# Score products with the keys' lo parts in a plane per head, over all 128 rows

## The chip, the cores and the metric

The kernel runs on one core of a Trainium2 chip, as one launch. The metric is the device time of one execution in microseconds, lower is better; the number given for a kernel is the median of its runs. The engines named here are TensorE (PE, with its weight loads shown apart as PEld), VectorE (DVE), ScalarE (ACT), GpSimd (POOL) and SyncE (SP), which issues most transfers.

## What is computed

Two decoder layers over 512 tokens of width 1024. Layer A is a gated short convolution, layer B a stick-breaking attention of 12 heads of 64 over keys and values made once; each layer also attends into 256 memory tokens with 4 heads of 64, and ends in a SwiGLU FFN. What the change touches are the two score products. In the reference they are:

```python
def memory_cross_attention(q, mem_k, mem_v):
    scale = 1.0 / math.sqrt(HEAD_DIM)
    s = jnp.einsum("bshd,bmhd->bhsm", q.astype(jnp.float32), mem_k.astype(jnp.float32)) * scale
    p = jax.nn.softmax(s, axis=-1)
...
def stick_breaking_attention(q, k, v):
    ...
        z = jnp.einsum("bhtd,bhsd->bhts", qb, kb) * scale
        log_not = jnp.where(causal, jax.nn.log_sigmoid(-z), 0.0)
        tail = lax.cumsum(log_not, axis=3, reverse=True) - log_not
        log_a = jax.nn.log_sigmoid(z) + tail
        a = jnp.where(causal, jnp.exp(log_a), 0.0)
        outs.append(jnp.einsum("bhts,bhsd->bhtd", a, vb))
```

## The kernel before

Every float32 operand of a product is held as two parts, hi (rounded to float32r) and lo (the rest), and a product is hi·hi + hi·lo + lo·hi, summed in PSUM. `mm` (L131 to 136) issues one matmul; all matmuls have line 132 in the profile, all transpositions line 139. `hi_of` (L143) makes a hi part on ScalarE and `lo_of` (L146) a lo part on VectorE.

A head has 64 features, so two heads share the 128 rows of a tile. `queries` (L414) writes for each head a plane `q[:, head]` of 128 rows: the head's own 64 rows hold the hi part, the other head's 64 rows hold the lo part. `keys` (L425) writes `kd[:, head]`, the hi part of the head's keys in both halves of the rows, and `kl`, the lo part, one plane in which each head has its own 64 rows. `scores_of` (L435) then makes a head's scores with two matmuls: queries (hi and lo) times `kd` over 128 rows, and queries hi times `kl` over the head's 64 rows alone.

`scores_of` has two callers. In `mem_attention`, `scores` makes for one head two token tiles of 256 memory scores, so four matmuls `sc` in a row; there are 8 such steps in each of the two layers. In layer B, `weigh` makes the scores `z` of one head and one query tile of 128 rows against 128, 256, 384 or 512 keys: two matmuls of `scores_of` and a third of 128 columns that adds the causal mask (`maskr`, `identr`, 128 rows). There are 12 heads of 4 query tiles, 48 steps. After `weigh`, ScalarE makes two sigmoids (L731, L732), VectorE a scan and a product (L734, L735), `turn` transposes the weights two steps later (`at`), and `weighted` multiplies them with the values (`av`).

The order of the work is a list of emission. `Lanes` counts columns of matmuls: a step of attention is put between the matmuls of a large product when so many columns have gone by (`STICK_PACE`, `MEM_PACE`), however long they took. Each engine then runs its list in order. The columns of both matmuls of `scores_of` are the same before and after the change. `kl` comes from a rotating pool of 3 buffers; the memory keys `k` of a pair are one tile of 3 planes (two of `kd`, one of lo). POOL has little to do: constants, the power -0.5 of each norm (`rstd_of`, L260) and the two zero columns ahead of each convolution input (`cu`, L565).

Of the kernel before, what the change touches and what calls it, by code (L numbers as in the profile page):

```python
# [9 lines left out]
F32 = mybir.dt.float32  # L10
F32R = mybir.dt.float32r
# [5 lines left out]
P = 128  # L17
# [15 lines left out]

# buffers
A_BUFS = 25
W_BUFS = 9
RAW_BUFS = 2
T_BUFS = 9
# column pairs of the FFN's hidden features that are held at a time
FF_GROUPS = ((0, 4), (4, 8), (8, 11))  # L40
# pieces of a weight that are held to finish one token tile after the other
TAIL = 3
# columns of matmuls between the steps of a generator (see Lanes)
STICK_PACE = 4900
MEM_PACE = 12000, 10000
TURN_PACE = 600
# columns of matmuls before a step that needs what other engines make
LAG_OUT = 8000
# [4 lines left out]
LAG_SECOND = 3000  # L53
# steps by which the transposition and the weighted sum of stick-breaking follow the weights
TURN_AFTER = 2
# [3 lines left out]
class Lanes:  # L59
    """Order of emission: generators whose steps are put between the matmuls of the large products.  # L60
    A step yields how many columns of matmuls are to come before its next one."""

# [40 lines left out]
def trunk(ctx: ExitStack, tc: tile.TileContext, x, mem, mix_norm, a_in, conv_w, b_in,  # L103
          kv_norm, w_kv_shared, w_mem_kv, w_o, ffn_norm, w_gate, w_up, w_down,
          mem_norm, final_norm, out):
    """Every float32 operand of a large product is held as two parts of 12 significant bits,
    hi = float32r(v) and lo = v - hi (exact), and a product is hi*hi + hi*lo + lo*hi, summed in
    float32 in PSUM."""
    nc = tc.nc
# [37 lines left out]

# [1 line left out]
    nw = [0]  # L149
# [21 lines left out]
    def cols(w, c0, raw=None):  # L171
        """w[:, c0:c0+256] -> two (hi, lo) pairs of 128 columns"""
        raw = load_cols(w, c0) if raw is None else raw
        return [lambda h=h: split(raw[:, :, h * P:(h + 1) * P], KT, P) for h in range(2)]

    def rows(w, pieces, c0, n):
        """pieces of consecutive row tiles of w[:, c0:c0+n], two pieces to a raw tile"""
        for i in range(0, len(pieces), 2):
            two = pieces[i:i + 2]
            nk = len(two[0])  # L180
            raw = raw_tile([P, 2 * nk, n])
            if len(two) == 2 and two[1][0] == two[0][-1] + 1:
                spans = [(0, two[0] + two[1])]
            else:
                spans = [(j * nk, kts) for j, kts in enumerate(two)]
            for at, kts in spans:
                nc.sync.dma_start(raw[:, at:at + len(kts), :],
                                  w[kts[0] * P:(kts[-1] + 1) * P, c0:c0 + n].rearrange("(k p) c -> p k c", p=P))
            for j, kts in enumerate(two):
                yield kts, split(raw[:, j * nk:j * nk + len(kts), :], len(kts), n)  # L190
# [5 lines left out]

# [1 line left out]
    ident = const.tile([P, P], F32, name="ident")  # L198
# [26 lines left out]
    def columns(src, n, name):  # L225
        """[n, 128] -> [128, n]"""
        b = att(f"tr_{name}")
        transpose(b[:, :n], src, ident[:n, :n])
        c = const.tile([P, n], F32, name=name)
        nc.vector.tensor_copy(c, b[:, :n])  # L230
        return c
# [6 lines left out]
    def load_table(func, after):  # L238
        """have ACT fetch the function's table once it has made `after`"""
        nc.scalar.activation(small.tile([P, 1], F32, tag="table", name=f"table_{func}"), after, func)  # L240

# [1 line left out]
    def sum_tile(name):  # L243
        return small.tile([P, 2], F32, tag="ss", name=f"ss_{name}")

    def square_sum(ss, xrow, hf, name, dve=False):
        """mean square, half of it"""
        row = xrow[:, hf * 512:(hf + 1) * 512]
        junk = tpool.tile([P, 512], BF16, tag="junk", name=f"junk_{name}{hf}", bufs=2)
        if dve:  # L250
            nc.vector.scalar_tensor_tensor(junk, row, 1.0 / D, row, ALU.mult, ALU.mult,
                                           accum_out=ss[:, hf:hf + 1])
        else:
            nc.scalar.activation(junk, row, AF.Square, scale=1.0 / 32.0, accum_out=ss[:, hf:hf + 1])
# [8 lines left out]
    class Feat:  # L263
        """[features, tokens], split, in tiles of 1024 columns"""

# [9 lines left out]
    class Normed:  # L275
        """feat = transposed (source * rstd) * gain for each (feat, gain) of `into`, two token tiles
        at a time"""

# [48 lines left out]

# [1 line left out]
    def three(dst, a, b, first, last):  # L329
        """dst (+)= a.T @ b for split a, b: each a function of HI, LO"""  # L330
        mm(dst, a(HI), b(HI), first, False)
        mm(dst, a(HI), b(LO), False, False)
        mm(dst, a(LO), b(HI), False, last)

    def by_feature(dst, w, feat, lo, hi):
        """dst[128 out, tokens lo:hi] = w.T @ feat"""
        for k in range(KT):
            three(dst, lambda hl: w[hl][:, k, :], lambda hl: feat.at(k, hl, lo, hi), k == 0, k == KT - 1)
            lanes.pump()

    class Opening:
        """the first four products on a feat whose token tiles come one after the other"""

# [20 lines left out]
    def by_token(w, pieces, c0, n, lhs, ntok, name, done, tail=1):  # L364
        """[tokens, n] = lhs.T @ w[:, c0:c0+n]; done(t, bank) at a token tile's end. The last
        `tail` pieces go token by token."""
        banks = [acc(f"{name}{t}") for t in range(ntok)]
# [17 lines left out]

# [1 line left out]
    def normed(t, src, into, name, dve):  # L387
# [25 lines left out]
    def queries(b, name):  # L413
        """two heads' queries, scaled, for matmuls over 128 rows: [:, head] = hi and lo of its 64 rows,  # L414
        hi at the head's own rows"""
        q = slot([P, 2, S], F32R, name)
# [8 lines left out]
    def keys(b, kd, kl):  # L425
        """two heads' keys: kd[:, head] = hi of its 64 rows, twice; kl = lo"""
        for hh in range(2):
            r = hh * HD
            own, other = slice(r, r + HD), slice(HD - r, P - r)
            hi_of(kd[own, hh, :], b[own, :])  # L430
            hi_of(kd[other, hh, :], b[own, :])
            lo_of(kl[own, :], b[own, :], kd[own, hh, :])

    def scores_of(dst, q, hh, t, kd, kl, last):
        """dst[token tile t, keys] = queries . keys of head hh"""  # L435
        own = slice(hh * HD, (hh + 1) * HD)
        mm(dst, q[:, hh, t * P:(t + 1) * P], kd, True, False)
        mm(dst, q[own, hh, t * P:(t + 1) * P], kl[own, :], False, last)

    def mem_kv(layer):  # L440
# [3 lines left out]
        for c, get in enumerate(cols(w, 0)):  # L444
            b = acc(f"mk{layer}{c}")
            by_feature(b[:, :M], get(), memT, 0, M)
            k = slot([P, 3, M], F32R, f"mk{layer}{c}")
            keys(b[:, :M], k[:, 0:2, :], k[:, 2, :])
            mk.append(k)
# [9 lines left out]

# [1 line left out]
    def stacked_pv(pv, r, yf, name):  # L461
        """pv rows 0:64 hold V_hi, 64:128 V_lo products: yf[r:r+64] = their sum"""
        tmp = t2([P, S], F32, f"pv_{name}")
# [9 lines left out]
    def mem_attention(qs, layer, ys, pace):  # L473
# [3 lines left out]
        def scores(head, tp):  # L477
            pair, nm = head // 2, f"{layer}{head}{tp}"
            sc = att(f"sc{nm}")
            for u in range(2):  # L480
                t = 2 * tp + u
                scores_of(sc[:, u * M:(u + 1) * M], qs[pair], head % 2, t, mk[pair][:, head % 2, :],
                          mk[pair][:, 2, :], True)
            sc3 = sc.rearrange("p (u m) -> p u m", u=2)
# [55 lines left out]

# [1 line left out]
    ymain = [None] * PAIRS  # L542
# [42 lines left out]

# [1 line left out]
    def residual(t, hf, b, ss, name):  # L587
# [21 lines left out]
    def out_proj_late(layer, ys, last, opening, then):  # L609
        """as out_proj, the first row tiles before the last ones are there"""  # L610
        for hf in range(2):
# [83 lines left out]

# [1 line left out]
    qs = [None] * PAIRS  # L697
# [5 lines left out]
    def values(g4):  # L703
        """V of heads 4*g4 .. 4*g4+3"""
        def done(t, b):
# [13 lines left out]
    def stick(pace):  # L719
        weight, aT, pvs, yfs = {}, {}, {}, {}  # L720

        def weigh(p, hh, i):
            """stick-breaking weights of query tile i, [t, s]"""
            q, (kd, kl) = qs[p], ks[p]
            n, nm = (i + 1) * P, f"{p}{hh}{i}"
            z = att(f"z{nm}")[:, :n]
            scores_of(z, q, hh, i, kd[:, hh, :n], kl[:, :n], False)
            mm(z[:, i * P:n], identr, maskr, False, True)
# [66 lines left out]
    for c2 in range(3):  # L795
# [3 lines left out]
        for c, get in enumerate(cols(w_kv_shared, c2 * 256)):  # L799
# [3 lines left out]
            kd = slot([P, 2, S], F32R, f"kd{p}")  # L803
            kl = tpool.tile([P, S], F32R, tag="kl", name=f"kl{p}", bufs=3)
            keys(b, kd, kl)
# [59 lines left out]
```

## Time and profile before

| | |
|---|---|
| median of 3 runs | 1195.9 us (1195.87 to 1196.12) |
| span of the profiled execution | 1193.9 us |
| PE busy | 1176.0 us, 98% |
| PEld busy | 986.9 us, 83% |
| DVE busy | 587.5 us, 49% |
| ACT busy | 478.9 us, 40% |
| POOL busy | 16.8 us, 1% |
| granted TensorE clock, mean | 0.998 |

A row of TensorE says when a matmul started and how long it took from there until its end; matmuls overlap, so what one costs the engine is the distance from its start to the start of the next. PEld is the load of the stationary operand that a matmul needs first. Times of day are us from the start of the span. Stick-breaking runs from about 664 to 810 us, the memory attention of layer A from 74 to 128 us, that of layer B from 603 to 650 us.

### The profile page before, as it was taken

What the parts mean: (1) busy time and instruction counts of PE and PEld (TensorE: products, weight loads), DVE (VectorE), ACT (ScalarE), POOL (GpSimd) and SP (SyncE); (2) the same over time, 40 slices, a digit from 0 to 9 for tenths busy, and PEclk for the clock granted to TensorE, in tenths of its full rate; (3) what the DMA queues carried; (4) which work ended last, traced back from release to release, by engine and by line L of the source; (5) the groups of instructions that cost most, each with busy time, mean ns of one, the idle gap of its engine ahead of it and who ended that gap; (6) DMA issues with size and microseconds to landing.
All of it is one profiled execution on the core that took longest, in us unless ns stands there. A gap on an engine that the chain in (4) does not pass through costs nothing.

```text
span 1193.9 us, 14463 instructions
## 1 busy us (share of the span) xinstructions
PE 1176.0 (98%) x5945; PEld 986.9 (83%) x5945; DVE 587.5 (49%) x853; ACT 478.9 (40%) x824; POOL 16.8 (1%) x37
## 2 busy tenths in 40 slices
PE   6999999999999999999999999999999999999997
PEld 6887888988888888888978888778988888888886
DVE  6657543533323333333777688887333333333334
ACT  7454523532213221223766576656332223222222
POOL 1000000000000000000000000001000000000000
PEclk9999999999999999999999999999999999999999
DMA  7332322242232422323231211022233242332321
GB/s 248 107 106 71 108 105 71 72 141 99 79 106 71 129 83 92 119 71 106 71 106 39 71 51 54 28 79 88 72 106 106 71 124 88 106 106 71 106 71 71
DMA packets 91118, 109.50 MB, mean 92 GB/s; under 512 B 2026, under 2 KB 73772, under 8 KB 91052
## 3 DMA queue, kind: packets, MB, share of 16 engines
q1 hardware_dynamic: 91019, 108.56, 28.0%
q8 instruction: 47, 0.77, 0.3%
q14 instruction: 20, 0.16, 0.0%
q10 hardware_dynamic: 32, 0.01, 0.0%
HBM read 106.46 MB, written 2.10 MB: 91 GB/s over the span
## 4 chain that ended last, share of the span: by engine, by line
PE 96%; ACT 1%; DVE 1%; issue 1%; POOL 0%; DMA 0%; POOLq 0%; SPq 0%; DVEq 0%; ACTq 0%
PE u L132 21%; PE d L132 20%; PE g L132 18%; PE o L132 6%; PE gu L132 3%; PE z L132 3%; PE v L132 3%; PE k L132 3%; PE bg L132 3%; PE q L132 2%; PE pb L132 2%; PE cg L132 2%; PE sc L132 1%; PE pa L132 1%; PE av L132 1%; PE at L139 1%
## 5 line engine op out<-in xcount | busy, mean ns | idle before, releaser
L146 DVE TENSOR_TENSOR wl<-raw,wh 128x1024 fp32r<-128x1024 f32 x196 | 239.8, 1224 | 437.7 <-PE u L132 178.5
L143 ACT ACTIVATE wh<-raw 128x1024 fp32r<-128x1024 f32 x196 | 207.5, 1060 | 385.3 <-PE d L132 101.8
L132 PE MATMUL d<-wh,hid 128*128 128x512 f32 x704 | 218.0, 389 | 0.0
L132 PEld LDWEIGHTS d<-wh,hid 128*128 128x128 f32 x704 | 132.2, 188 | 27.3
L132 PE MATMUL d<-wl,hid 128*128 128x512 f32 x352 | 136.9, 389 | 0.0
L132 PEld LDWEIGHTS d<-wl,hid 128*128 128x128 f32 x352 | 66.1, 188 | 13.7
L656 ACT ACTIVATE sg<-g 128x512 f32<-128x512 f32 x40 | 24.0, 600 | 117.2 <-PE g L132 117.2
L132 PE MATMUL g<-hffn0h,wh 128*128 128x512 f32 x160 | 62.3, 389 | 0.0
L132 PE MATMUL g<-hffn1h,wh 128*128 128x512 f32 x160 | 62.3, 389 | 0.0
L132 PE MATMUL g<-hffn0l,wh 128*128 128x512 f32 x160 | 62.3, 389 | 0.0
L132 PE MATMUL g<-hffn1l,wh 128*128 128x512 f32 x160 | 62.3, 389 | 0.0
L132 PE MATMUL g<-hffn0h,wl 128*128 128x512 f32 x160 | 62.2, 389 | 0.0
L132 PE MATMUL u<-hffn0h,wh 128*128 128x512 f32 x160 | 62.2, 389 | 0.0
L132 PE MATMUL u<-hffn0l,wh 128*128 128x512 f32 x160 | 62.2, 389 | 0.0
L132 PE MATMUL u<-hffn0h,wl 128*128 128x512 f32 x160 | 62.2, 389 | 0.0
L132 PE MATMUL g<-hffn1h,wl 128*128 128x512 f32 x160 | 62.2, 389 | 0.0
L132 PE MATMUL u<-hffn1h,wh 128*128 128x512 f32 x160 | 62.2, 389 | 0.0
L132 PE MATMUL u<-hffn1l,wh 128*128 128x512 f32 x160 | 62.2, 389 | 0.0
L132 PE MATMUL u<-hffn1h,wl 128*128 128x512 f32 x160 | 62.2, 389 | 0.0
L146 DVE TENSOR_TENSOR hid<-sg,hid 128x512 fp32r<-128x512 f32 x44 | 30.5, 693 | 33.3 <-ACT hid L143 33.3
L589 DVE TENSOR_TENSOR x<-d,x 128x512 f32<-128x512 f32 x48 | 33.1, 690 | 25.7 <-PE d L132 25.7
L734 DVE TENSOR_TENSOR_SCAN sn<-sn 128x127 f32<-128x127 f32 (+3 forms) x48 | 39.2, 818 | 13.4 <-ACT sn L731 12.7
(242 smaller groups left out, 2355.9 us busy)
## 6 DMA issues: line engine op xcount, KB each, us to landing
raw<-in_w_gate_dram SPq DMA_DIRECT2D x22, 1024.0 KB, 5.4
raw<-in_w_up_dram SPq DMA_DIRECT2D x22, 1024.0 KB, 5.5
raw<-in_w_down_dram SPq DMA_DIRECT2D x20, 1024.0 KB, 5.0
raw<-in_a_in_dram SPq DMA_DIRECT2D x8, 1024.0 KB, 5.1
raw<-in_w_o_dram SPq DMA_DIRECT2D x12, 512.0 KB, 3.9
raw<-in_w_kv_shared_dram SPq DMA_DIRECT2D x6, 1024.0 KB, 5.0
raw<-in_w_mem_kv_dram SPq DMA_DIRECT2D x4, 1024.0 KB, 5.1
raw<-in_b_in_dram SPq DMA_DIRECT2D x4, 1024.0 KB, 5.0
```

The costliest lines, as they stand in the source:

```text
L132: nc.tensor.matmul(dst, a, b, start=start, stop=stop)
L139: nc.tensor.transpose(dst, src, idn)
L143: nc.scalar.activation(dst, src, AF.Copy)
L146: nc.vector.tensor_tensor(dst, src, hi.bitcast(F32), ALU.subtract)
L589: nc.vector.tensor_tensor(part, b, part, ALU.add)
L656: nc.scalar.activation(sg, bg, AF.Silu)
L734: nc.vector.tensor_tensor_scan(back, back, back, 1.0, ALU.mult, ALU.bypass)
```

## The change

The lo part of the keys gets a plane per head, like the hi part: in plane `kl[:, head]` the head's own 64 rows hold the lo part and the other head's rows hold zeros. The second matmul of `scores_of` then takes the whole 128 rows of `q[:, head]` and of that plane; the lo parts of the queries, which stand in the other rows, meet zeros. The zeros are written once by POOL (`zero_rows`). In layer B three tiles of two planes (`key_lo`) are made ahead of the loop and used in turn; for the memory keys the tile `k` grows from 3 to 4 planes, and each of its four instances gets two MEMSETs. Comments that were dropped are left out of the diff.

```diff
+KL_BUFS = 3
...
     def keys(b, kd, kl):
...
-            lo_of(kl[own, :], b[own, :], kd[own, hh, :])
+            lo_of(kl[own, hh, :], b[own, :], kd[own, hh, :])
 
     def scores_of(dst, q, hh, t, kd, kl, last):
-        own = slice(hh * HD, (hh + 1) * HD)
         mm(dst, q[:, hh, t * P:(t + 1) * P], kd, True, False)
-        mm(dst, q[own, hh, t * P:(t + 1) * P], kl[own, :], False, last)
+        mm(dst, q[:, hh, t * P:(t + 1) * P], kl, False, last)
+
+    def zero_rows(kl):
+        for hh in range(2):
+            nc.gpsimd.memset(kl[HD - hh * HD:P - hh * HD, hh, :].bitcast(F32), 0.0)
...
-            k = slot([P, 3, M], F32R, f"mk{layer}{c}")
-            keys(b[:, :M], k[:, 0:2, :], k[:, 2, :])
+            k = slot([P, 4, M], F32R, f"mk{layer}{c}")
+            zero_rows(k[:, 2:4, :])
+            keys(b[:, :M], k[:, 0:2, :], k[:, 2:4, :])
...
-                          mk[pair][:, 2, :], True)
+                          mk[pair][:, 2 + head % 2, :], True)
...
+    key_lo = [const.tile([P, 2, S], F32R, name=f"kl{i}") for i in range(KL_BUFS)]
+    for kl in key_lo:
+        zero_rows(kl)
...
-            scores_of(z, q, hh, i, kd[:, hh, :n], kl[:, :n], False)
+            scores_of(z, q, hh, i, kd[:, hh, :n], kl[:, hh, :n], False)
...
-            kl = tpool.tile([P, S], F32R, tag="kl", name=f"kl{p}", bufs=3)
+            kl = key_lo[p % KL_BUFS]
```

The lists of PE, DVE, ACT and SP hold the same instructions in the same places before and after; only POOL's list changes, at two places. At the start of the program, POOL makes the powers for the norms of the four token tiles (`rstd_x0` to `rstd_x3`) and of the two memory tiles (`rstd_m0`, `rstd_m1`); a bracket names the engines (or the DMA queue) whose signal a row waits for. Before:

```order
L260 TENSOR_TENSOR rstd_x0_128<-ms_x0_126,minus_half_82 128x1 [waits DVE_49]
L260 TENSOR_TENSOR rstd_x1_140<-ms_x1_138,minus_half_82 128x1 [waits DVE_49]
L260 TENSOR_TENSOR rstd_x2_196<-ms_x2_194,minus_half_82 128x1 [waits DVE_49]
L260 TENSOR_TENSOR rstd_x3_208<-ms_x3_206,minus_half_82 128x1 [waits DVE_49]
L260 TENSOR_TENSOR rstd_m0_468<-ms_m0_466,minus_half_82 128x1 [waits DVE_49]
L260 TENSOR_TENSOR rstd_m1_480<-ms_m1_478,minus_half_82 128x1 [waits DVE_49]
```

After:

```order
L261 TENSOR_TENSOR rstd_x0_128<-ms_x0_126,minus_half_82 128x1 [waits DVE_49]
L261 TENSOR_TENSOR rstd_x1_140<-ms_x1_138,minus_half_82 128x1 [waits DVE_49]
L444 MEMSET kl0_4337 64x512 [waits Pool_49]
L444 MEMSET kl0_4337 64x512
L444 MEMSET kl1_4338 64x512 x2
L444 MEMSET kl2_4339 64x512 x2
L261 TENSOR_TENSOR rstd_x2_196<-ms_x2_194,minus_half_82 128x1 [waits DVE_49,Pool_49]
L261 TENSOR_TENSOR rstd_x3_208<-ms_x3_206,minus_half_82 128x1 [waits DVE_49]
```

The six MEMSETs of the layer-B planes, though written far down in the program, stand between the powers of the second and the third token tile. In layer A, POOL's list holds the zero columns `cu` of the six convolution inputs; before:

```order
L565 MEMSET cu1_601 128x2
L565 MEMSET cu2_1018 128x2 [waits DVE_49,PE_49]
L565 MEMSET cu3_1075 128x2 [waits DVE_49,PE_49]
L565 MEMSET cu4_1478 128x2 [waits DVE_49]
L565 MEMSET cu5_1513 128x2 [waits PE_49,Pool_49]
```

After, the MEMSETs of the memory keys `mk` stand among them (`mk00`, `mk01` of layer A, `mk10`, `mk11` of layer B):

```order
L572 MEMSET cu1_601 128x2
L444 MEMSET mk00_707 64x256 [waits Pool_49]
L444 MEMSET mk00_707 64x256
L444 MEMSET mk01_745 64x256 [waits PE_49,Activation_49]
L444 MEMSET mk01_745 64x256
L572 MEMSET cu2_1022 128x2 [waits DVE_49,PE_49,Pool_49]
L572 MEMSET cu3_1079 128x2 [waits DVE_49,PE_49]
L444 MEMSET mk10_1269 64x256 [waits DVE_49,DMAHW6_49,PE_49,Pool_49]
L444 MEMSET mk10_1269 64x256
L444 MEMSET mk11_1318 64x256 [waits PE_49]
L444 MEMSET mk11_1318 64x256
L572 MEMSET cu4_1486 128x2 [waits DVE_49,Pool_49]
```

Two `cu` now stand behind the MEMSETs of `mk00` and `mk01`, and two behind those of `mk10` and `mk11`; the waits in the `mk` rows are for their slots to come free.

## Rows read from the trace of the kernel before

**Rows 1.** The page's first part: busy time of an engine in us, its share of the span, and its instructions.

```profile
PE 1176.0 (98%) x5945; PEld 986.9 (83%) x5945; DVE 587.5 (49%) x853; ACT 478.9 (40%) x824; POOL 16.8 (1%) x37
```

**Rows 2.** The page's fourth part, the chain of work that ended last: shares of the span by engine.

```profile
PE 96%; ACT 1%; DVE 1%; issue 1%; POOL 0%; DMA 0%; POOLq 0%; SPq 0%; DVEq 0%; ACTq 0%
```

**Rows 3.** The timeline, one score step of stick-breaking with 512 keys: start in us, duration in us, engine (PEld is the weight load of the product that follows it), line, operation, tiles, rows*columns of the array and the operand's shape, count, and in brackets idle time of that engine before it.

```profile
672.14 0.39 PE L132 MATMUL z<-kd,q 128*128 128x512 f32 x1
672.46 0.18 PEld L132 LDWEIGHTS z<-kl,q 64*128 64x128 f32 x1 [0.25 <-issue]
672.46 0.49 PE L132 MATMUL z<-kl,q 64*128 64x512 f32 x1
...
672.88 0.33 PE L132 MATMUL z<-maskr,identr 128*128 128x128 f32 x1
...
673.05 0.41 PE L139 MATMUL at<-ident,sp 128*128 128x128 f32 x2
```

**Rows 4.** The timeline of TensorE alone, same columns: a step with 256 keys and the product ahead of it; then the first product and the transposition behind the last one of a step with 128 keys (789.64) and of one with 384 keys (793.34).

```profile
677.68 0.28 PE L132 MATMUL v<-wh,hkvl 128*128 128x256 f32 x1
677.80 0.28 PE L132 MATMUL z<-kd,q 128*128 128x256 f32 x1
678.01 0.38 PE L132 MATMUL z<-kl,q 64*128 64x256 f32 x1
678.32 0.33 PE L132 MATMUL z<-maskr,identr 128*128 128x128 f32 x1
678.49 0.51 PE L139 MATMUL at<-ident,sp 128*128 128x128 f32 x3
...
789.64 0.22 PE L132 MATMUL z<-kd,q 128*128 128x128 f32 x1
...
790.21 0.52 PE L139 MATMUL at<-ident,sp 128*128 128x128 f32 x3
...
793.34 0.34 PE L132 MATMUL z<-kd,q 128*128 128x384 f32 x1
...
794.15 0.30 PE L139 MATMUL at<-ident,sp 128*128 128x128 f32 x1
```

**Rows 5.** The view of one tile, the stick-breaking scores `z`: engine, operation, count, then minimum, median and maximum duration in ns, first and last start in us, and the forms with their counts (array rows*columns, moving operand).

```profile
L132 PE MATMUL z<-kd,q x48: 220/333/397, 664.8 to 796.8; 128*128 128x128 f32 x12, 128*128 128x256 f32 x12, 128*128 128x384 f32 x12, 128*128 128x512 f32 x12
...
L132 PE MATMUL z<-kl,q x48: 323/410/496, 664.9 to 797.1; 64*128 64x128 f32 x12, 64*128 64x256 f32 x12, 64*128 64x384 f32 x12, 64*128 64x512 f32 x12
```

**Rows 6.** The timeline of TensorE around one step of the memory attention's scores `sc` (its four products are one row, x4), and from the view of the tile `sc` the counts of its products in layer A (`qm_a`) and layer B (`qm_b`).

```profile
602.97 0.40 PE L132 MATMUL q<-hmix1l,wh 128*128 128x512 f32 x1
603.20 0.39 PE L132 MATMUL q<-hmix1h,wl 128*128 128x512 f32 x1
603.43 1.22 PE L132 MATMUL sc<-mk,qm_b 128*128 128x256 f32 x4
604.58 0.50 PE L132 MATMUL q<-hmix1h,wh 128*128 128x512 f32 x1
604.91 0.40 PE L132 MATMUL q<-hmix1l,wh 128*128 128x512 f32 x1
...
L132 PE MATMUL sc<-mk,qm_a x32: 276/381/387, 74.4 to 116.7; 128*128 128x256 f32 x16, 64*128 64x256 f32 x16
...
L132 PE MATMUL sc<-mk,qm_b x32: 276/381/387, 603.4 to 639.6; 128*128 128x256 f32 x16, 64*128 64x256 f32 x16
```

**Rows 7.** Busy time by windows, from the first score step of one head to that of the next (twelve heads, 664.79 to 800.70): length, then busy us and instructions of PE, PEld, DVE, ACT and POOL, the granted clock, the DMA share, GB/s. The fourth and the eighth head, and the sum of all twelve.

```profile
699.24:710.12 10.88, 10.88 (x71) 9.06 (x70) 10.58 (x18) 8.35 (x19) 0.00 (x0) 1.00 0.05 11
...
744.68:755.76 11.08, 11.08 (x59) 8.57 (x58) 10.27 (x18) 9.03 (x19) 0.00 (x0) 1.00 0.01 3
...
sum 135.91, PE 135.34 PEld 109.25 DVE 113.69 ACT 89.16 POOL 0.00; mean PE 11.28 PEld 9.10 DVE 9.47 ACT 7.43 POOL 0.00
```

**Rows 8.** The view of waits between 660 and 830 us: who waited for whom, us in total, times, the longest in us.

```profile
DVE sn L734 <- ACT sn L731: 12.7, 19, 1.8
DVE kl L146 <- ACT kd L143: 5.6, 6, 1.6
...
PE at L139 <- ACT sp L732: 0.6, 1, 0.6
```

**Rows 9.** The timeline at two transpositions `at` of stick-breaking weights, with the VectorE product `sp` that makes the weights: the first one of the stage (670.22), and the one of pair 1, head 0, last query tile (701.78).

```profile
669.81 0.61 DVE L735 TENSOR_TENSOR sp<-sp,sn 128x127 f32<-128x127 f32 x2
...
670.22 0.30 PE L139 MATMUL at<-ident,sp 128*128 128x128 f32 x1 [0.57 <-ACT sp L732]
...
700.72 0.68 DVE L735 TENSOR_TENSOR sp<-sp,sn 128x511 f32<-128x511 f32 x1
...
701.78 0.62 PE L139 MATMUL at<-ident,sp 128*128 128x128 f32 x4
```

**Rows 10.** POOL: its timeline in the first 20 us, and from the groups by line that of the small MEMSETs (count, busy us, mean ns of one, idle time before them and what ended it).

```profile
0.73 0.20 POOL masks.py:197 MEMSET ident<- 128x128 f32 x1 [0.29 <-POOLq L852]
...
6.77 1.50 POOL L260 TENSOR_TENSOR rstd_x<-ms_x,minus_half 128x1 f32<-128x1 f32 x2 [5.07 <-DVE ms_x L258]
13.79 0.55 POOL L260 TENSOR_TENSOR rstd_x<-ms_x,minus_half 128x1 f32<-128x1 f32 x1 [5.53 <-DVE ms_x L258]
...
L565 POOL MEMSET cu<- 128x2 f32 x6 | 0.5, 100 | 90.4 <-PE pt L139 66.8 <-DVE ya L146 23.6
```

## The prediction

> **What bounds the kernel now.** I read the page's busy times first: PE is busy 98% of the span, no other engine half of it [rows 1]. The chain of work that ended last says the same of the path: 96% of it is PE [rows 2]. So what the end depends on is how many microseconds TensorE needs for its list, and a change that saves time there is worth its full size unless PE then has to wait. The next question is whether the touched matmuls cost more than their columns, and for that the starts in the timeline are the thing to read, not the durations, because matmuls overlap.
>
> The normal price: a 256-column product over 128 rows starts 0.12 us after the one before it (677.68 to 677.80, [rows 4]), a 512-column one 0.23 us (602.97 to 603.20 to 603.43, [rows 6]). A 128-column one is limited by its weight load: four transpositions in a row take 0.62 us where one takes 0.30, so (0.62 - 0.30)/3 = 0.11 us each [rows 9]. A 384-column one is not to be seen in a plain stream; I take the middle of 0.12 and 0.23, 0.175.
>
> The touched products are dearer. In the 512-key step [rows 3] `z<-kd` starts at 672.14; the weight load of `z<-kl`, which uses 64 rows, begins only at 672.46, with an idle PEld before it, together with its own matmul. The mask product, 128 rows again, starts 0.42 us later, and the transposition 0.17 after that. So the weight load for a product of 64 rows doesn't run beside the product of 128 rows ahead of it, nor the load for 128 rows beside the one of 64 rows. The price is paid twice in a step: on the way in and on the way out.
>
> **The change, part by part.**
>
> *Stick-breaking scores.* There are 48 steps, 12 of each width [rows 5]. From the start of `z<-kd` to the start of the transposition behind the mask, a step takes now: 128 keys 790.21 - 789.64 = 0.57; 256 keys 678.49 - 677.80 = 0.69; 384 keys 794.15 - 793.34 = 0.81 [rows 4]; 512 keys 673.05 - 672.14 = 0.91 [rows 3]. With three products over 128 rows at the normal price it would take 3 x 0.11 = 0.33; 0.12 + 0.12 + 0.11 = 0.35; 0.175 + 0.175 + 0.11 = 0.46; 0.23 + 0.23 + 0.11 = 0.57. Saved: 0.24, 0.34, 0.35, 0.34, together 1.27 us for a head, x 12 heads = 15.2 us.
>
> *Memory scores.* Each of the 16 steps is four products in a row, with 128, 64, 128, 64 rows ([rows 6]: 16 + 16 products in each layer, four to a step). The step shown begins at 603.43, and the second large product behind it starts at 604.91; the first one behind it (0.33 instead of 0.23) still pays for the way back to 128 rows. That is 1.48 us; at the normal price it is 4 x 0.12 + 0.23 = 0.71. Saved 0.77 x 16 = 12.3 us. PE's list becomes 27.5 us shorter in all.
>
> *What PE then waits for.* Steps are placed by columns, and columns stay the same, so the other engines have that much less time between a score and the transposition that needs it. Weights are split far ahead and matter little; the short loop is score, sigmoids, scan, product `sp`, transposition. The first transposition of the stage already waits: PE idle 0.57 us ahead of 670.22 ([rows 9]; the row blames ACT's `sp`, but VectorE's `sp` rows end right there; [rows 8] has the same wait). Two scores lie between it and its own score, the 256- and the 384-key one, so 0.69 us of the saving turns into waiting there. At 701.78 VectorE's `sp` had ended at 700.72 + 0.68 = 701.40, 0.38 us earlier [rows 9]; the two scores between are the 128- and the 256-key ones, 0.58 us shorter, so PE waits 0.2. Then VectorE's throughput: from one head's first score to the next head's, PE would need 1.27 us less. VectorE is busy 10.58 us in the fourth head, which would shrink from 10.88 to 9.61, an excess of 0.97; in the eighth 10.27 against 11.08 - 1.27 = 9.81, an excess of 0.46; in the sum 113.7 us against 135.9 - 15.2 = 120.7, so it fits on the whole and an excess can be made good by the next head [rows 7]. Loss between 0.9 us (the two named waits) and 0.9 + 0.97 + 0.46 = 2.3 us (each excess paid in full). I take 1.7, nearer the upper end, since an engine this full queues; not the end itself, since the 0.38 us of slack at 701.78 shows that PE doesn't wait for each excess at once.
>
> *POOL.* Fourteen MEMSETs are added, on an engine that is off the path. A MEMSET of 128 columns takes 0.20 us, one of 2 columns 0.10 [rows 10], so 0.83 ns a column; 512 columns are 0.10 + 0.43 = 0.53 us, six of them 3.2 us. They stand in POOL's list behind the second power, which ends at 6.77 + 1.50 = 8.27, and ahead of the third, which began at 13.79 after 5.53 us of idling [rows 10]. The gap covers them with 2.3 us left. If the cover were gone the price would be what they are late by, since the third and fourth token tile wait for these powers. Bounds: from 6 x 0.10 = 0.6 us (width costs nothing) to some 7 us if a column cost twice as much, which is 1.5 us late. I take 0. The eight MEMSETs of the memory keys, about 0.10 + 256 x 0.83 ns = 0.31 us each, 2.5 us in all, stand ahead of two pairs of `cu`; POOL idled 90.4 us ahead of the six `cu`, waiting for buffers and not for time [rows 10]. The score product itself now waits for POOL too, for a MEMSET that stands behind such long idling. I take 0.
>
> *No cost.* `keys` writes the same 12 lo parts to other places; ACT, DVE and SP do the same work in the same order. One weight load per product stays.
>
> Sum: 27.5 - 1.7 = 25.8 us. The span would go from 1193.9 to 1168.1. What lies around it is 1195.9 - 1193.9 = 2.0 us against the median, and stays. **Predicted: 1195.9 - 25.8 = 1170.1 us.**
>
> **The rivals.**
>
> (a) *VectorE and ScalarE set the pace in stick-breaking.* VectorE's idle time there isn't all free: it waits 12.7 us for `sn` and 5.6 us for `kd` of ScalarE [rows 8]. If those waits don't shrink with PE's list, VectorE needs 113.7 + 18.3 = 132.0 of the 135.9 us, and the stage saves only 3.9 instead of 15.2: 1195.9 - 12.3 - 3.9 = 1179.7. For it: VectorE at 93% to 97% of the shortened heads above. Against: these waits follow PE's scores, which come earlier, and ScalarE has 9.03 us in its fullest head [rows 7], less than 9.81. A part of this is likelier than the whole.
>
> (b) *The load stays unhidden.* If two products over the same rows couldn't overlap load and stream, each touched product and the one behind would still pay 0.11 us for its load. A `z` step then costs three loads and its bare streams (0.11 for 256 columns, 0.22 for 512): 0.49, 0.60, 0.71, 0.82, a gain of 0.08, 0.09, 0.10, 0.09, x 12 = 4.3 us; an `sc` step 4 x 0.22 + 0.22 + 0.11 = 1.21, a gain of 0.27 x 16 = 4.3 us. Time 1187.3. The Trainium skill ("TensorE: Matmul & The Clock Gate", Part 3) says that a weight load overlaps a running matmul only where the row groups differ, which speaks for this rival and against the change. Against it stand the stream rows: 128-row products follow each other at 0.12 and 0.23 us [rows 4, 6], with a load for each of them [rows 1].
>
> (c) *It doesn't do what it says.* If the gaps belonged to the sum in one PSUM bank or to the lo plane's place, nothing would change: 1195.9. Against: `sc` pays twice more at the pair's second 128-row product and at the plain product behind it, which has another bank.
>
> (d) *Slower.* The MEMSETs at the start hold up the third power. To eat the 25.8 us beyond the 5.5 us of cover, one would have to take (25.8 + 5.5)/6 = 5.2 us, ten times my 0.53; at 6 us each the time is 1195.9 - 25.8 + 36 - 5.5 = 1200.6. Only POOL's rough spans speak for it.
>
> **How the numbers follow.** The forecast, 1167.5 to 1174, has 0.70: its upper end holds the 2.3 us of loss and a start late by 1.5 us, with some queueing at VectorE's high load; its lower end a loss near 0.9 and normal prices a tenth below mine. Rival (a), from 1174 to 1180, 0.16; (b) 0.04; (c) 0.03; (d) 0.02; below 1167.5, 0.05. For 8 in 10 the range reaches over the nearer part of (a): 1167.5 to 1177. A measurement of this kernel can tell about 0.2%, 2.4 us, from no change; faster by more has 0.95, within it 0.03, slower 0.02.
>
> **What would show it.** In the new profile the `z<-kl` and half of the `sc` rows read 128*128; the four `z` distances are near 0.33, 0.35, 0.46, 0.57, and an `sc` step with the product behind it near 0.71; the idle time of PEld ahead of `z<-kl` is gone. PE's busy time falls by about 27 us, and PE idles about 2 us in stick-breaking, at 670 and around 700 first. If that idling is near 10 us, (a) holds; if the distances stay above 0.5 for 256 keys, (b) or (c). If the third power starts after 14 us, the MEMSETs are dearer than costed.

## The result and the profile after

1170.28 us (median of 4 runs, 1170.02 to 1170.4) against 1195.91: the ratio is 0.9785, interval 0.9773 to 0.9797. The profiled execution spans 1168.6 us where that of before spans 1193.9. 1170.1 was forecast.

The page's busy times and the chain by engine, after:

```profile
PE 1147.8 (98%) x5945; PEld 982.5 (84%) x5945; DVE 584.9 (50%) x853; ACT 477.3 (41%) x824; POOL 23.1 (2%) x51
...
PE 93%; DVE 3%; ACT 2%; issue 1%; DMA 0%; POOL 0%; POOLq 0%; SPq 0%; DVEq 0%; ACTq 0%
```

PE's busy time fell by 28.2 us with the same 5945 matmuls [rows 1]; the chain holds 93% PE in place of 96% [rows 2], the rest having gone to DVE and ACT. That is where the new waits show, and they are taken up below.

The step with 512 keys, timeline, answering to [rows 3]:

```profile
670.30 0.40 PE L133 MATMUL z<-kd,q 128*128 128x512 f32 x1
670.30 0.19 PEld L133 LDWEIGHTS z<-kl,q 128*128 128x128 f32 x1
...
670.53 0.40 PE L133 MATMUL z<-kl,q 128*128 128x512 f32 x1
...
670.76 0.22 PE L133 MATMUL z<-maskr,identr 128*128 128x128 f32 x1
...
670.83 0.39 PE L140 MATMUL at<-ident,sp 128*128 128x128 f32 x2
```

The weight load of `z<-kl` now starts with the matmul ahead of it, at 670.30; before, it started 0.32 us behind it. From `z<-kd` to the transposition: 0.53 us, before 0.91. The steps with 256, 128 and 384 keys on TensorE, answering to [rows 4]:

```profile
665.34 0.28 PE L133 MATMUL z<-kd,q 128*128 128x256 f32 x1
...
665.63 0.62 PE L140 MATMUL at<-ident,sp 128*128 128x128 f32 x4
...
765.49 0.22 PE L133 MATMUL z<-kd,q 128*128 128x128 f32 x1
765.55 0.28 PE L133 MATMUL z<-kl,q 128*128 128x128 f32 x1
765.66 0.28 PE L133 MATMUL z<-maskr,identr 128*128 128x128 f32 x1
765.77 0.52 PE L140 MATMUL at<-ident,sp 128*128 128x128 f32 x3
...
768.51 0.33 PE L133 MATMUL z<-kd,q 128*128 128x384 f32 x1
...
768.91 0.28 PE L140 MATMUL at<-ident,sp 128*128 128x128 f32 x1
```

0.29, 0.28 and 0.40 us; before 0.69, 0.57 and 0.81. The memory step, answering to [rows 6]:

```profile
597.65 0.64 PE L133 MATMUL sc<-mk,qm_b 128*128 128x256 f32 x4
598.12 0.39 PE L133 MATMUL q<-hmix1h,wh 128*128 128x512 f32 x1
598.35 0.39 PE L133 MATMUL q<-hmix1l,wh 128*128 128x512 f32 x1
```

From 597.65 to 598.35 it is 0.70 us, before 1.48; and the product behind the step is followed after 0.23 us (598.12 to 598.35).

The same matmuls' starts in the two traces, subtracted, give the account by stage: at the first memory scores of layer A the new kernel is 0.41 us late (74.19 to 74.60); behind them 5.77 us early (135.08 to 129.31); ahead of layer B's memory scores 5.79 (602.01 to 596.23) and behind them 11.79 (645.01 to 633.22); behind stick-breaking 25.70 (815.09 to 789.39), and this stays to the last matmul; the spans differ by 25.3, since the transfer of the output behind it ends 0.4 us later in the new profile. So: start -0.4, memory scores 6.2 + 6.0, stick-breaking 13.9.

The waits between 645 and 815 us on TensorE (PEld rows are the same waits seen at the weight load):

```profile
PEld at L140 <- ACT sp L742: 2.6, 3, 1.8
...
PEld z L133 <- DVE aTl L147: 1.6, 5, 0.8
...
PE at L140 <- DVE sp L745: 1.6, 1, 1.6
```

Those for `at` are for weights that aren't made yet, that of `z` for a PSUM bank that VectorE still reads. The largest is ahead of the first transposition of the stage:

```profile
656.36 0.28 ACT L741 ACTIVATE sn<-z 128x128 f32<-128x128 f32 x1
...
658.43 0.30 PE L140 MATMUL at<-ident,sp 128*128 128x128 f32 x1 [1.62 <-DVE sp L745]
```

Its score step begins at 653.00 and takes 0.28 us, but ScalarE copies keys and a weight tile from 652.85 to 656.34 without a break and makes the first sigmoid only then. How another wait comes about, in order of time (pair 1, head 0, last query tile; answering to the second half of [rows 9]):

```profile
680.04 1.20 ACT L144 ACTIVATE kd<-k 64x512 fp32r<-64x512 f32 x2 [0.90 <-PE k L133]
...
680.99 0.23 PE L133 MATMUL z<-maskr,identr 128*128 128x128 f32 x1
...
681.26 1.06 ACT L144 ACTIVATE wh<-raw 128x1024 fp32r<-128x1024 f32 x1
...
682.35 1.20 ACT L144 ACTIVATE kd<-k 64x512 fp32r<-64x512 f32 x2
...
683.57 0.60 ACT L741 ACTIVATE sn<-z 128x512 f32<-128x512 f32 x1
...
684.31 1.22 DVE L744 TENSOR_TENSOR_SCAN sn<-sn 128x511 f32<-128x511 f32 x1
...
685.90 0.68 DVE L745 TENSOR_TENSOR sp<-sp,sn 128x511 f32<-128x511 f32 x1
...
686.73 0.63 PE L140 MATMUL at<-ident,sp 128*128 128x128 f32 x4
```

The scores are done soon after 680.99 + 0.23. ScalarE, which makes the sigmoids, has two pairs of key copies with a weight tile between them ahead in its list, until 683.57. Scan and product follow on VectorE, which is through at 686.58, and the transposition starts at 686.73. Most of the lateness, 2.3 us, is ScalarE's list; VectorE adds some 0.5 us, with a lo part of keys ahead of the scan and one of attention weights (`aTl`) ahead of the product. And the start of the program, answering to [rows 10]:

```profile
8.67 3.50 POOL L444 MEMSET kl<- 64x512 f32 x6
14.23 0.55 POOL L261 TENSOR_TENSOR rstd_x<-ms_x,minus_half 128x1 f32<-128x1 f32 x1 [2.06 <-DVE ms_x L259]
...
8.65 0.83 DVE L288 TENSOR_SCALAR xn_hmix<-x,rstd_x 128x512 f32<-128x512 f32 x1
```

The six MEMSETs take 3.50 us (3.2 were costed) and the third power begins 2.06 us behind them, so the cover held. The power does start after 14 us, which the prediction took for a sign of dearer MEMSETs; but it waits for VectorE's `ms_x` and not for POOL. VectorE's normalization beside the MEMSETs took 0.83 us, before 0.49.

### The profile page after: what moved, and what is told of

The parts are those of the page before. It is cut to its first block, busy times and chain, and to the rows that moved or that the text cites. A ratio compares the mean times of both kernels' runs of the same rounds, so it can differ in the third digit from the quotient of the medians.

```text
span 1168.6 us, 14482 instructions
## 1 busy us (share of the span) xinstructions
PE 1147.8 (98%) x5945; PEld 982.5 (84%) x5945; DVE 584.9 (50%) x853; ACT 477.3 (41%) x824; POOL 23.1 (2%) x51
## 4 chain that ended last, share of the span: by engine, by line
PE 93%; DVE 3%; ACT 2%; issue 1%; DMA 0%; POOL 0%; POOLq 0%; SPq 0%; DVEq 0%; ACTq 0%
PE u L133 21%; PE d L133 20%; PE g L133 19%; PE o L133 6%; PE gu L133 3%; PE bg L133 3%; PE v L133 2%; PE pb L133 2%; PE q L133 2%; PE k L133 2%; PE cg L133 2%; PE pa L133 1%; PE z L133 1%; PE av L133 1%; PE mv L133 1%; PE mk L133 1%
```

## The experiments

**Each half alone.** Planes and MEMSETs as in the changed kernel; `scores_of` chooses the rows by its caller (`last` is true for the memory scores only).

```diff
-        mm(dst, q[:, hh, t * P:(t + 1) * P], kl, False, last)
+        rows = slice(0, P) if last else slice(hh * HD, (hh + 1) * HD)
+        mm(dst, q[rows, hh, t * P:(t + 1) * P], kl[rows], False, last)
```

> The changed kernel with planes and MEMSETs as they are, but only the memory scores run over all 128 rows; the stick-breaking scores take the head's own 64 rows of the plane. If the gain is the sum of the two score products' own savings (my theory): the memory part alone, 16 steps of 0.77 us, some 12.2 us off, time 1184. If the two gains overlap (one of them only fills idle time of the other engines, rival), less than 10 us or more than 15 us off: above 1186 or below 1181.

1184.5 us, ratio 0.9905 (0.989 to 0.992). The other way round (`rows` of the head's own 64 where `last` is true):

> The mirror image: only the stick-breaking scores run over 128 rows, the memory scores over 64. The sum theory: 25.6 - 12.2 = 13.4 us off, time 1182.5, with the same waits of TensorE in stick-breaking as in the changed kernel, about 4 us. The rival that the stage is at VectorE's pace whatever TensorE does would show fewer than 10 us off: above 1186.

1182.52 us, ratio 0.9889 (0.9874 to 0.9904). 11.3 and 13.3 us off. Both pay the 0.4 us for planes and MEMSETs (next run), the change only once: 11.3 + 13.3 + 0.4 = 25.0 beside its 25.6, so the two gains add to within 0.6 us. The stick-breaking stage saves 13.9 us in the trace of the half alone as in that of the change, with the same waits.

**Planes without the rows.** Both lo products over `rows = slice(hh * HD, (hh + 1) * HD)` of the new planes.

> Planes per head and all MEMSETs as in the changed kernel, but both lo products run over the head's own 64 rows, as before. If the rows of the array make the price (my theory): no gain, 1195.9 to 1196.5, the upper end if the MEMSETs at the start cost the 0.4 us by which the changed kernel's first score step comes later. If the place of the lo part makes it (rival): near 1170.

1196.17 us, ratio 1.0003 (0.9994 to 1.0013), no gain. The rows of the array make the price; the place of the lo part does not, and rival (c) is out.

**What is paid for, a row change or a product of 64 rows?** The kernel before, with the hi product over 64 rows as well:

```diff
-        mm(dst, q[:, hh, t * P:(t + 1) * P], kd, True, False)
+        mm(dst, q[own, hh, t * P:(t + 1) * P], kd[own], True, False)
```

> The kernel before, but the hi product of the scores too runs over the head's own 64 rows; it leaves out the product of the queries' lo part with the keys' hi part. If the price is one of changing the rows between neighbours (my theory), a memory step then has two changes in place of four and falls from 1.48 to about 1.1 us, inside it the products follow each other at 0.12 us, and a stick-breaking step keeps its two: 16 x 0.38 = 6 us off, time 1190. If each product of 64 rows pays by itself (rival), inside a memory step they follow at 0.31 us, and the time is 1198 to 1205.

1189.6 us, ratio 0.9949 (0.9932 to 0.9966). TensorE around one memory step of layer A:

```profile
74.11 0.39 PE L132 MATMUL cg<-hmix0h,wl 128*128 128x512 f32 x1
74.43 0.74 PE L132 MATMUL sc<-mk,qm_a 64*128 64x256 f32 x4
75.10 0.50 PE L132 MATMUL cg<-hmix0h,wh 128*128 128x512 f32 x1
75.44 0.40 PE L132 MATMUL cg<-hmix0l,wh 128*128 128x512 f32 x1
```

Four 64-row products and the way back, 74.43 to 75.44, take 1.01 us; with 0.09 on entry (74.11 to 74.43 is 0.32 in place of 0.23) 1.10, as expected, where before it was 1.48. Taken apart, the four start at 74.43, 74.65, 74.77 and 74.90: the first is followed after 0.22 us, the others after 0.12 to 0.13, as cheaply as products of 128 rows.

The kernel before, the memory step's products reordered: both 128-row ones first, then both 64-row ones.

```diff
-            for u in range(2):
-                t = 2 * tp + u
-                scores_of(sc[:, u * M:(u + 1) * M], qs[pair], head % 2, t, mk[pair][:, head % 2, :],
-                          mk[pair][:, 2, :], True)
+            hh = head % 2
+            own = slice(hh * HD, (hh + 1) * HD)
+            for part in range(2):
+                for u in range(2):
+                    t = 2 * tp + u
+                    dst = sc[:, u * M:(u + 1) * M]
+                    if part == 0:
+                        mm(dst, qs[pair][:, hh, t * P:(t + 1) * P], mk[pair][:, hh, :], u == 0, False)
+                    else:
+                        mm(dst, qs[pair][own, hh, t * P:(t + 1) * P], mk[pair][own, 2, :], False, u == 1)
```

> The kernel before, with its 64-row lo products, but in a memory step the two products over 128 rows come first and the two over 64 rows behind them. If the price belongs to each change of rows between neighbours (my theory), a step has two changes in place of four: half of the 0.77 us a step, 16 x 0.39 = 6.2 us off, time 1189.7. If it belongs to each 64-row product (rival), nothing: 1195.8.

1189.93 us, ratio 0.995 (0.9937 to 0.9964), as expected. The step on TensorE:

```profile
74.46 0.82 PE L132 MATMUL sc<-mk,qm_a 128*128 128x256 f32 x4
75.21 0.50 PE L132 MATMUL cg<-hmix0h,wh 128*128 128x512 f32 x1
75.55 0.40 PE L132 MATMUL cg<-hmix0l,wh 128*128 128x512 f32 x1
```

74.46 to 75.55 is 1.09 us, with the same 64-row products as the 1.48 of before. The price is one per change of rows between neighbours, on the way in and on the way out, and a reordering alone gets half of the memory part's gain without any plane.

**Where the saving in stick-breaking is lost.** First the length of the loop: `TURN_AFTER` 2 to 3 and `SUM_AFTER` 5 to 6 in the changed kernel.

> The changed kernel with the transposition and the weighted sum of stick-breaking each one step later, so that a score has one step more to become weights. TensorE waits some 4 us in the changed kernel's stick-breaking stage. If these waits come from the length of the loop score, sigmoids, scan, product (my theory), more than half of them go: 1167 to 1168.5. If VectorE's throughput sets them (rival), they only move to another place: 1170.

1172.55 us, 2.3 us slower than the change and above both forecasts. TensorE's waits in that run:

```profile
PE z L133 <- DVE aTl L147: 1.6, 2, 1.4
PE o L133 <- DVE kl L147: 1.4, 1, 1.4
...
PE ol L133 <- ACT ys L144: 0.6, 1, 0.6
PE o L133 <- DVE ys L147: 0.6, 1, 0.6
```

The waits of the transpositions for weights are gone, so the length of the loop had a part in them; but in their place TensorE waits 1.6 us for banks, 2.3 for banks and results in the output projection and 0.6 for the last result. As a way to a shorter time the theory fell. Then the columns: the weights' lo parts times all 128 columns of the values, in stick-breaking and in the memory attention,

```diff
-                mm(pv[0:P if part == HI else HD, ip * 256 + s0:(ip + 1) * 256], value(j, head, part == HI),
+                mm(pv[:, ip * 256 + s0:(ip + 1) * 256], value(j, head, True),
...
-                mm(pv[0:HD, :], mv[:, m, head, HI, :], pt[LO][:, m, :], False, False)
+                mm(pv, both[:, m, :], pt[LO][:, m, :], False, False)
```

> The changed kernel, and the products of the attention weights' lo parts with the values use all 128 columns of the array (both parts of the values) in place of 64; it adds the lo times lo part that was left out. If a change of columns between neighbours has a price as a change of rows has, 0.08 us on entry are gone for 24 groups in stick-breaking and 0.07 for 8 in the memory attention, 2.5 us; the load of 128 columns in place of 64 ahead of 24 short products of 128 columns costs 0.05 each, 1.2 us back: 1169. If the columns have no such price (rival): 1171 to 1171.5.

1170.46 us, no different from the change (1170.28), between the two forecasts. The distances from the start ahead of a sum of eight products to the second start behind it are alike in both traces (median 1.16 and 1.17 us), and so is each distance inside: the first product is followed after 0.20 us whether the next has 64 or 128 columns. A change of columns has no price here. And both edits:

> Both of the last two edits on the changed kernel. If they are independent: the sum of their gains, some 1167. If TensorE's saving in the sums only becomes waiting for VectorE: no better than the later transposition alone, 1167.5 to 1168.5.

1172.58 us, as the later transposition alone and above both forecasts; since the columns save nothing by themselves, this run doesn't tell the two apart.

Then VectorE's load. The 4.2 us of waiting that the next forecasts start from count 1.5 us (`tr_hffn` and `gu`) behind the stage, which the kernel before waits as well. The lo parts of the weight tiles (from the second group of values on to the output projection) go to POOL:

```diff
-        lo_of(l, raw, h)
+        lo_on[0].tensor_tensor(l, raw, h.bitcast(F32), ALU.subtract)
...
+        if c2 == 1:
+            lo_on[0] = nc.gpsimd
```

> The changed kernel, but in stick-breaking the lo parts of 14 weight tiles are made by POOL in place of VectorE; TensorE needs them 16 us and more after VectorE makes them. The later transposition showed that TensorE's waits there (4.2 us) only move when the loop gets a step more. If VectorE's load makes them (my theory now), 17 us less of it leave fewer than 1.5 us of waiting: 1167.5. If the rotation of four PSUM banks or ScalarE makes them (rival): 1170. If POOL slows VectorE where both work on SBUF (second rival): 1171 or more.

1179.61 us, 9.3 us slower than the change: the second rival (see the last section). Without POOL, `split` returning the hi tile twice:

> The changed kernel, but the same 14 lo parts are not made by any engine; TensorE multiplies with the hi part in their place, so its list keeps its length, and the output leaves those lo parts out. VectorE's load alone is lowered, without POOL. VectorE's load as the cause: 1167 to 1168, waits under 1.5 us. PSUM banks or ScalarE as the cause: 1170.

1169.63 us, between the forecasts, 0.65 less than the change with runs that touch (1169.58 to 1170.29 against 1170.02 to 1170.4). And ScalarE's load, `split` taking one ready tile (`ym[0]`) as every hi part:

> The changed kernel, but in stick-breaking the hi parts of the same 14 weight tiles are not made by ScalarE; one tile of the memory attention's result stands in their place, in TensorE's products and in VectorE's lo parts, so that the lists of TensorE and VectorE keep their length and the output is that of other weights. Without VectorE's lo parts 3.0 of the 4.2 us of waiting stayed. If ScalarE's list makes them (my theory now: at 681 us the copies of keys and of a weight tile, 3.5 us in a row, stand ahead of the sigmoids of a score that is done by 681.2), fewer than 2 us of waiting are left: 1167.5 to 1168.5. If the rotation of the PSUM banks makes them (rival): 1170.

1167.9 us, ratio 0.9766 (0.9752 to 0.978), 2.4 us less than the change and clear of it. Busy times between 653 and 780 us, the columns as in [rows 7], first the change, then without VectorE's lo parts, then without ScalarE's hi parts:

```profile
653.00:780.00 127.00, 124.01 (x815) 111.88 (x814) 114.83 (x196) 90.52 (x204) 0.00 (x0) 1.00 0.18 59
```

```profile
653.00:780.00 127.00, 125.13 (x821) 112.89 (x820) 105.64 (x187) 88.39 (x201) 0.00 (x0) 1.00 0.13 43
```

```profile
653.00:780.00 127.00, 126.12 (x827) 114.13 (x826) 114.26 (x196) 81.12 (x194) 0.00 (x0) 1.00 0.13 42
```

TensorE's idle time is 2.99 us with the change, 1.87 with VectorE's load lowered and 0.88 with ScalarE's, though VectorE is as busy in the last (114.26) as with the change (114.83). At the place shown above, ScalarE's list in the last run reads:

```profile
678.91 1.20 ACT L144 ACTIVATE kd<-k 64x512 fp32r<-64x512 f32 x2 [0.90 <-PE k L133]
680.13 0.60 ACT L749 ACTIVATE sn<-z 128x512 f32<-128x512 f32 x1
680.63 0.59 ACT L750 ACTIVATE sp<-z 128x512 f32<-128x512 f32 x1
681.25 1.20 ACT L144 ACTIVATE kd<-k 64x512 fp32r<-64x512 f32 x2
```

The two sigmoids start at 680.13, behind one pair of key copies. So the larger part of the waiting goes with the weight copies that stand ahead of sigmoids in ScalarE's list; VectorE's lo parts take about a third of the idle time and a quarter of that gain in time, in part the same microseconds. The last run doesn't part the two cleanly: without the hi tiles VectorE's lo parts have no copy to wait for either, and fewer buffers of the weight pool are in use. VectorE's own list is seen in one wait, the 0.8 us ahead of the score product at 737.43, whose bank waits for an `aTl` that stands behind a weight tile, keys, scan and product on VectorE; it is gone in both runs. What is left, some 1.3 us, wasn't taken apart.

**The start.** The memory half alone on the kernel before, without the layer-B tiles and their MEMSETs.

```diff
-            k = slot([P, 3, M], F32R, f"mk{layer}{c}")
+            k = slot([P, 4, M], F32R, f"mk{layer}{c}")
...
-        mm(dst, q[own, hh, t * P:(t + 1) * P], kl[own, :], False, last)
+        own = slice(0, P) if last else slice(hh * HD, (hh + 1) * HD)
+        mm(dst, q[own, hh, t * P:(t + 1) * P], kl[own], False, last)
```

> The kernel before with only the memory scores over 128 rows, and without the three layer-B tiles and their six MEMSETs at the start (the first experiment had them). If these tiles and MEMSETs cost the 0.4 us at the start, x lands by 5.86 us on the span as before and the time is 1183.8 to 1184.1; if the later start has another reason (rival): 1184.4 as in that experiment, with x landing near 6.2 us.

1183.97 us, 0.5 less than with them (1184.5), and VectorE's first work on the second tile of x starts at 5.85 us, as in the kernel before (5.86; with the change 6.20). By the medians the tiles and MEMSETs together cost that half microsecond, though the runs touch (1183.86 to 1184.15 against 1184.1 to 1184.69). Of how much the longer normalization beside the MEMSETs is the cause stays open: it takes 0.83 us in all nine traces with the six MEMSETs and 0.49 in the four without, but the first work on the second tile of x, which comes ahead of the MEMSETs, starts anywhere from 5.91 to 6.22 in the nine and from 5.78 to 5.92 in the four.

No version here that computes the whole output is faster than the change. Moving ScalarE's copies behind the sigmoids in its list wasn't tried; leaving 14 of the weight copies out gained 2.4 us, and what moving them, or the key copies, would gain is open.

## Why the prediction was right

By its own steps:

- *What bounds the kernel* and *rows make the price*: right. The price sits at the changes of rows, as [rows 3] suggested; planes without full rows gain nothing, and regrouping gains half in the memory scores.
- *Memory scores*, 12.3 us: 12.2 measured (6.2 + 6.0).
- *Stick-breaking*, 15.2 us ahead of waits: mis-sized. By the steps shown it is (0.57 - 0.28) + (0.69 - 0.29) + (0.81 - 0.40) + (0.91 - 0.53) = 1.48 us a head; the medians of the same step's saving in both traces, over all twelve heads, are 0.286, 0.384, 0.391 and 0.384, together 1.445 a head and 17.3 us in all. The term that was wrong is the 0.11 us for every 128-column product, read from transpositions in a row. Behind a wider product the load of a 128-column one is hidden and it adds some 0.06 (765.49 to 765.55, 670.76 to 670.83).
- *PE's waits*, 1.7 us from bounds of 0.9 to 2.3: too small, 17.3 - 13.9 = 3.4. Beside the two named places the bounds counted VectorE's fullness alone. Those two were right in kind: at the first transposition of the stage TensorE waits 1.06 us more (0.69 said), at 701.78 in the old trace 0.17 more (0.2 said), though another 0.38 is lost one step ahead of it. What was missing is ScalarE's list; "weights are split far ahead and matter little" was the step that failed. At the first transposition the copies, and not its score, set when ScalarE begins, so the saving of all three steps ahead of it turns into waiting (0.29 + 0.39 + 0.39 = 1.07), and not of two.
- *POOL*, 0: right but for half a microsecond with the tiles, which isn't the powers' doing; by what way it comes isn't shown. The upper bound was added up wrongly and mattered nowhere: at twice the price a column, six MEMSETs are 6 x 0.95 = 5.7 us and not 7, 0.2 us late and not 1.5.

The sum came out within 0.2 us because the first miss (2.1 us too little gain) and the second and the start (1.7 + 0.4 too little cost) cancel. That it is so close is luck. The time was right; two of its terms were not.

Rival (a) held in part: it had 11.3 us lost, and 3.4 were. The 93% to 97% named for it are VectorE's shares of the heads before (10.27 of 11.08, 10.58 of 10.88); of the shortened ones they are 105% and 110%, so more spoke for it than was said. Rival (b) is out: products over the same rows overlap load and stream, 128 after 128 and 64 after 64, and it is at a change of rows that they don't. The Trainium skill's sentence that it rested on ("TensorE: Matmul & The Clock Gate", Part 3: a weight load overlaps a running matmul only where the row groups differ) is not what these runs show: `z<-kl` loads 128 rows beside a product over the same 128 rows (670.30), and the load for 64 rows between 128-row ones waits (672.46 in the old trace). "TensorEngine Tiling (Array Packing)", Key Properties, says that a change of the tiling mode drains the engine; for rows the two regrouping runs agree that a change costs time, about 0.2 us a way (0.77 us for four), while for 64 columns between 128 the run with full columns shows no price.

## What to carry to other kernels

Read what a small matmul costs from the distance of starts, and look at its neighbours: on a full TensorE a product over part of the rows cost here 0.14 to 0.2 us each time the rows changed (0.286 to 0.391 for two changes, 0.77 for four), so fill the other rows with zeros, or put products of one shape side by side. Then ask of every engine in the loop, not only of the busiest, what stands in its list ahead of the work that TensorE will now ask for sooner: a saving of 17.3 us in a stage kept 13.9. A forecast that hits can rest on two misses; hold each term against the trace.

## What the runs showed of the hardware

In the run with weight lo parts on POOL, VectorE stands still for POOL where both read SBUF. Groups by line between 653 and 780 us, the change first, then that run:

```profile
L745 DVE TENSOR_TENSOR sp<-sp,sn 128x383 f32<-128x383 f32 x12 | 6.6, 547 | 0.1
```

```profile
L747 DVE TENSOR_TENSOR sp<-sp,sn 128x383 f32<-128x383 f32 x11 | 9.9, 904 | 0.1
...
L147 DVE TENSOR_TENSOR aTl<-at,aTh 128x384 fp32r<-128x384 f32 x11 | 6.0, 550 | 0.0
```

The product, both inputs in SBUF, goes from 547 to 904 ns in the mean; `aTl`, one input of which is in PSUM, keeps its 550 (551 with the change). The mean hides that most products take their usual time and a few wait POOL out. One of them, from the timeline:

```profile
691.65 2.59 POOL L162 TENSOR_TENSOR wl<-raw,wh 128x1024 fp32r<-128x1024 f32 x1 [7.85 <-PE k L133]
...
692.14 2.51 DVE L747 TENSOR_TENSOR sp<-sp,sn 128x383 f32<-128x383 f32 x1
```

POOL ends at 694.24, the product at 694.66. In stick-breaking nine VectorE instructions with both inputs in SBUF (scans, products, a lo part of `ys`) begin while POOL works, and each ends its own usual time, less some 0.14 us, behind POOL's end. The Trainium skill ("SBUF — State Buffer", Who interferes with whom) says that a VectorE instruction with two SBUF inputs contends with a POOL instruction that reads SBUF, and that scalings in a two-port mode contend with any; the first agrees with these rows. The 0.83 us of the scaling beside the MEMSETs fits the second; that the scaling is in such a mode isn't shown.

The same run shows what TensorE lost on top of a wait of 1.91 us (ahead of 699.22, for a bank), by windows:

```profile
696.00:700.00 4.00, 2.09 (x20) 1.94 (x19) 3.73 (x8) 3.01 (x8) 0.00 (x0) 1.00 0.31 114
700.00:704.00 4.00, 4.00 (x24) 4.00 (x22) 3.62 (x8) 2.07 (x6) 0.00 (x0) 0.59 0.00 0
```

PE is busy 2.09 of 4 us, and in the next 4 us the granted clock is 0.59 in the mean, so it stood at the lower of its two levels (1.2 in place of 2.4 GHz) for most of them; a 256-column product is then followed after 0.21 us (701.01 to 701.22) in place of 0.12. With the change itself the granted clock is 1.00 from 653 to 780 us, with its shorter waits.
